# A new order of issue: measured lengths in the planner's list, and every stage's seeds searched anew

## The chip, the cores and the metric

The kernel runs on one core of a Trainium2 chip. Its engines are TensorE (PE, with PEld for its weight loads), VectorE (DVE), ScalarE (ACT), GpSimd (POOL) and SyncE (SP), which issues most of the DMAs. The metric is the device time of one execution, in microseconds (us).

## The reference

Two blocks in a row over 512 tokens of width 1024, in float32. Cut to what is computed:

```
hl = modulate(rms_norm(x), sh1, sc1)          # sh, sc, gt from silu(c) @ w_ada (24 MB)
q, k, v, f = split(hl @ w_in)                 # rope on q, k; 256 context rows join k, v
a = softmax(q1 k1) - lam * softmax(q2 k2)     # differential attention, 4 heads
mix = [rms_norm(a v), real(fft2(f)) @ w_fourier]   # 4 Fourier groups
x = x + gt1 * (mix @ w_out)
x = x + gt2 * hier_moe(modulate(rms_norm(x)))  # 32 experts, top 2 of 8 in one group, SwiGLU of 512
x = rms_norm(x, g_final)
# second block
p = rms_norm(x) @ w_in_2                      # 1024 -> 6152 columns
o_sb = stick_breaking_attention(...) * silu(gate)      # 8 heads of 64
o_g = gated_delta_rule(conv(...)) * silu(gate)         # 4 heads of 128, chunks of 64
y = (sig(m1) * (o_sb @ w_sb) + sig(m2) * (o_g @ w_gdn)) @ w_out_2
x = x + rms_norm(y)
```

## The kernel before

The whole work is one program in six stages, each recorded and then put in order by a planner. The stages, with the number of recorded operations, are the projections (1160: modulation from `w_ada`, norms, `w_in`, rope), the attention (901: Fourier mix, differential attention, the products with `w_out`, the router's weights), a short second stage (285: router and first gathers), the MoE (1661: 16 pairs of experts; every expert's weights are streamed, 64 x 3 DMAs of 1 MB), and two tail stages for the second block (2076 and 1867). All products are float32 kept by three fp32r products: a matrix is split into a high part (`wh`, `mh`, `w2h`, `bh`) and a rest (`wl`, `ml`, `w2l`, `bl`), and high x high, high x low and low x high are summed in PSUM. The high part is a cast, the rest a subtraction on DVE of some 128x512 or 128x1024 elements.

The order of issue is neither written by hand nor left to a compiler. A `Recorder` stands in the place of the engines (`s.nc.tensor`, `s.nc.vector` and so on); each call is kept with its operands. At the end of a stage `flush` gives each operation a priority (`rank`: the longest chain of costs behind it), changes the priorities by a list of random moves, one seed each, and runs `plan`, a list scheduler that plays the engines, buffers and DMAs by estimated costs (`cost_of`). The order that comes out is issued as it stands; each engine then runs its own operations strictly in that order and waits where an operand isn't there. Some operations may go to either of two engines (`alts`), and the planner chooses. All recorded instructions therefore carry one line, L1126, but for pairs of 64-column products (L852) and two scaling helpers (L794, L802).

The seeds stand in `ORDERS`, one row for each stage: (number of operations, share, keep, look, shy, seeds). The costs used to rank and to plan also decide what every old seed leads to: the first stage's outcome is carried into the next (`Recorder.before`).

Names used below: `ada` are blocks of `w_ada` (1 MB each), `kT` and `qT` rows of x (512 KB each) and later keys and queries, `pm` the modulation products in PSUM, `sc` silu(c); `sp` attention scores, `mx` their row maximum on DVE, `p` the weights, `pt` their transposes; `pf`, `pe`, `po` products of the Fourier transform with the tables `ab` and `dft`; `wout` blocks of `w_out` with rest `wl`; `py` an expert pair's output, `yt` and `yl` its weighted copy and rest, `x1` the residual; `w2`, `w2h`, `w2l` blocks of the second block's `w_in_2`. After the MoE stage a loop for overfull experts stands outside the recorder (0 rounds here): DVE copies `rk` just ahead of it, and all engines meet at it.

Of the kernel before, what the change touches and what calls it, by code (L numbers as in the profile page):

```python
# [537 lines left out]
def front(s, tc, ins, ctx, x1st, second, dump=None):  # L538
# [69 lines left out]
    if dump: dump("attn")  # L608
# [45 lines left out]
)  # L654


# [43 lines left out]
def _count(ap):  # L700
    n = 1
    for _, c in ap.ap[1:]:
        n *= c
    return n


class Recorder:
# [7 lines left out]
    before = ({}, {})  # L715
    turn = 0

    rate, switch = 360, 0

    LAT = {"tensor": {"tensor": 0, "vector": 196, "scalar": 197},  # L720
           "vector": {"tensor": 256, "vector": 127, "scalar": 160, "gpsimd": 200},
# [20 lines left out]

    def cost(self, eng, method, out, ins, kw):
        x = self.cost_of(eng, method, out, ins, kw)
        if self.switch and eng in ("vector", "scalar") and any(_count(a) > 64 and abs(a.ap[-1][0]) > 1 for a in (out, *ins)):

            x *= 1.75 if eng == "vector" else 2
        return x

    def cost_of(self, eng, method, out, ins, kw):  # L750
        n = _count(out)
        psum = any(str(a.space).endswith("PSUM") for a in ins + [out])
        if eng == "tensor":
            lhs = ins[0]
            if method == "transpose":
                return max(ins[0].ap[0][1] / 1.2, 50) + 3
            m = _count(lhs)
            if "32r" in str(lhs.dtype):
                return max(n, 256) / 2.4 + 2
            if m <= 32:  # L760
                return 19 + 0.43 * n
            if m <= 64:
                return 26 + 0.834 * n
            return max(4 * n, 512) / 2.4
        if eng == "scalar":
            return 0.833 * n + (60 if psum else 100) + (90 if kw.get("accum_out") is not None else 0) + \
                (84 if not isinstance(kw.get("scale", 1.0), float) else 0) + (90 if not isinstance(kw.get("bias", 0.0), float) else 0)
        if eng == "vector":
            n = max([n] + [_count(a) for a in ins])
            if method == "tensor_reduce":  # L770
                n = _count(ins[0])
            fast = method in ("tensor_copy", "tensor_scalar", "memset") and not psum
            return (0.52 if fast else 1.04) * n + 65 + 63 * sum(_count(a) == 1 for a in ins if n > 1)
        if eng == "gpsimd":
            if kw.get("op") is not None and "pow" in str(kw["op"]):
                return 300 + 165 * n
            if method == "scalar_tensor_tensor":
                return 100 + 1.4 * n
            return 200 + 2.1 * n if method == "tensor_tensor" else 150 + 0.9 * n
        return 60  # L780
# [136 lines left out]
    def plan(self, keep, look=0, shy=0):  # L917
# [9 lines left out]
        free = {e: self.before[0].get(e, 0.0) for e in self.ENGINES}  # L927
# [10 lines left out]
        dma, order, cols, sent = self.before[0].get("dma", 0.0), [], {}, []  # L938
        slots = {k: [(0.0, ())] * b for k, b in self.psum.items()}
        parked = {k: [] for k in slots}  # L940
        left, has, used, tiled = {}, set(), {}, False
        nexts = {k: 0 for k in slots}
        while len(order) < len(ops):
            best = None
# [13 lines left out]
            t, e = best  # L958
# [5 lines left out]
            op = heapq.heappop(now[e] if now[e] else later[e])[2]  # L964
# [49 lines left out]
            if e == "tensor":  # L1014


                x = 0
                for ph in (0.0, 0.5):
                    n = int(t / self.TICK + ph)
                    if n and cols.get((ph, n - 1), 0) < 3060:  # L1020
                        x = op.alts[e][1]
                small = "tile_position" in op.kw
                free[e] += x + (self.switch * (tiled != op.mode) if self.switch else 85 * (tiled and not small))
                tiled = op.mode if self.switch else small
                for ph in (0.0, 0.5):
                    n = int(free[e] / self.TICK + ph)
                    cols[ph, n] = cols.get((ph, n), 0) + op.cols
# [365 lines left out]
def phase_moe(s, last):  # L1393
    tc, nc, i = s.tc, s.nc, s.i
    right = "right"

    def load(e0):
        return s.pre.pop(e0) if e0 in s.pre else prefetch(s, e0, ahead=False)

    with ExitStack() as st:  # L1400
        s.ringD = st.enter_context(tc.tile_pool(name="ringD", bufs=RING - 17, reuse_waits="tile"))
        xp = st.enter_context(tc.tile_pool(name="xm", bufs=2, side=right, reuse_waits="tile"))
        ps = st.enter_context(tc.tile_pool(name="ps_m", bufs=8, space=PSUM, reuse_waits="tile"))
        s.nc = Recorder(nc, tc)
        s.nc.rate, s.nc.switch = 360, 95
        for x in s.ring:
            s.nc.tile(x)
        for e0 in range(0, 32, 2):
            got = s.got.pop(e0, None)
            if got is None:  # L1410
                got = gather(s, e0, s.rank, s.gx, ps, s.xs[e0 // 2 % 2])
            moe_pair(s, e0, got, xp, ps, load)
        last()
        s.nc.flush()
        s.nc = nc

    with ExitStack() as st:
        xp = st.enter_context(tc.tile_pool(name="xg", bufs=1, side=right, reuse_waits="tile"))
        ps = st.enter_context(tc.tile_pool(name="ps_g", bufs=8, space=PSUM, reuse_waits="tile"))
        wl = xp.tile([128, 512], F32, name="wl")  # L1420
        rk = xp.tile([128, 4, 32], F32, name="rk")
        nc.vector.tensor_copy(rk, s.rank)
        n = nc.values_load(s.nrounds[0:1, 0:1], min_val=0, max_val=512)
        with tc.For_i(0, n, 1):
            nc.vector.tensor_scalar(rk, rk, -float(s.cap), None, OP.add)
            for e0 in range(0, 32, 2):
                def load1(e0):
                    def ws(m, k, a):

                        nc.sync.dma_start(wl, expert_views(s, e0 + a)[m][:, k])  # L1430
                        return wl
                    return ws
                got = gather(s, e0, rk, xp, ps, s.xs[1], 1)
                moe_pair(s, e0, got, xp, ps, load1, paired=False)
    Recorder.before = ({}, {})
# [731 lines left out]
```

## Time and profile before

| | |
|---|---|
| three runs | 1327.03, 1330.16, 1330.43 us; median 1330.16 |
| the profiled execution | 1329.8 us, of which the span of the trace is 1328.1 us and 1.7 us lie around it |
| PE busy | 1233.0 us, 93% of the span, 7067 matmuls |
| DVE busy | 803.1 us, 60%, 1602 instructions |
| ACT, POOL busy | 529.3 us (40%), 109.7 us (8%) |
| granted TensorE clock, mean | 0.971 of full speed |
| moved by DMA | 297.5 MB, 224 GB/s over the span |

Times are microseconds from the start of the span. A row of the timeline gives the start, the time from the first start to the last end of the merged instructions, the engine, line and operation, output and inputs, the count, and in brackets how long the engine had been idle before and what released it. Matmuls are pipelined: the next may start while the last one is still shown, so that the distance of the starts, the pitch, is what a product costs. A row of the stretches gives the stretch, its length, busy time and count for each engine, the granted clock, the DMA share and GB/s.

### The profile page before, as it was taken

To read this page: it belongs to the slowest core of one execution; us is meant where nothing else is said; L and a number is where in the kernel's file an instruction comes from. 1 tells how busy PE (TensorE), PEld (TensorE's weight loads), DVE (VectorE), ACT (ScalarE), POOL (GpSimd) and SP (SyncE) were. 2 spreads that over 40 slices of the span, in tenths; PEclk is the share of its full clock that TensorE was granted. 3 is DMA by queue.
4 is the path that set the end of the run, shared out by engine and by line. 5 is a ranking of instruction groups with operands and counts; after the bars stand their busy time and mean duration, and the time that the engine had idled before them with its cause. 6 is when DMAs were issued, how large, how long until landed. Compare 5 with 4: busy or idle time off the path is not lost. (4 is left out here: it accounts for less than half of the span.)

```text
span 1328.1 us, 18293 instructions
## 1 busy us (share of the span) xinstructions
PE 1233.0 (93%) x7067; PEld 795.7 (60%) x7067; DVE 803.1 (60%) x1602; ACT 529.3 (40%) x1053; POOL 109.7 (8%) x115
## 2 busy tenths in 40 slices
PE   5999989899689999979998997899999999999997
PEld 3778667767333444424443332678777878888776
DVE  5788999867233443524434335769555676778674
ACT  4645367312112221311213212367554647458521
POOL 1213230021000000000000000102000100000010
PEclk9999999899689999989999999899999999999999
DMA  9976240118999999999999996222212221222421
GB/s 342 327 258 204 88 132 1 64 64 344 382 370 419 419 420 418 418 418 420 420 420 419 418 419 239 76 64 95 65 34 65 65 64 64 69 90 78 157 69 63
DMA packets 94228, 297.52 MB, mean 224 GB/s; under 512 B 10939, under 2 KB 44836, under 8 KB 69558
## 3 DMA queue, kind: packets, MB, share of 16 engines
q1 hardware_dynamic: 90166, 287.87, 56.3%
q0 software_dynamic: 3392, 6.31, 1.4%
q10 hardware_dynamic: 576, 2.10, 0.4%
q8 instruction: 57, 0.93, 0.3%
q14 instruction: 37, 0.30, 0.1%
HBM read 294.14 MB, written 6.31 MB: 226 GB/s over the span
## 5 line engine op out<-in xcount | busy, mean ns | idle before, releaser
L852 PE MATMUL pgu<-we,xT 128*64 128x512 f32 x1024 | 233.6, 604 | 7.7 <-DMA we<-in_w_gate_dram 7.7
L852 PEld LDWEIGHTS pgu<-we,xT 128*64 128x64 f32 x1024 | 73.2, 139 | 151.2 <-issue 146.1
L852 PE MATMUL py<-we,hT 128*64 128x512 f32 x512 | 121.6, 614 | 12.8 <-DMA we<-in_w_down_dram 9.5
L1126 PE MATMUL pgm<-bh,w2h 128*128 128x512 f32 x352 | 131.4, 407 | 0.0
L1126 PE MATMUL pgm<-bl,w2h 128*128 128x512 f32 x352 | 129.1, 402 | 0.0
L1126 PE MATMUL pgm<-bh,w2l 128*128 128x512 f32 x352 | 129.0, 402 | 0.0
L1126 DVE TENSOR_TENSOR x<-x,po 128x512 f32<-128x512 f32 x152 | 96.7, 683 | 36.1 <-PE po L1126 35.6
L1126 DVE SCALAR_TENSOR_TENSOR yt<-py,gs,gt 128x512 f32<-128x512 f32 x32 | 24.0, 751 | 115.9 <-PE py L852 110.4
L852 PEld LDWEIGHTS py<-we,hT 128*64 128x64 f32 x512 | 36.0, 141 | 83.3 <-issue 64.6
L1126 ACT CAST yh<-yt 128x512 fp32r<-128x512 f32 x32 | 19.8, 618 | 149.9 <-DVE yt L1126 149.7
L1126 PEld LDWEIGHTS pgm<-bl,w2h 128*128 128x128 f32 x352 | 66.1, 189 | 14.2 <-issue 0.2
L1126 PEld LDWEIGHTS pgm<-bh,w2h 128*128 128x128 f32 x352 | 66.0, 189 | 13.7 <-issue 0.3
L1126 PEld LDWEIGHTS pgm<-bh,w2l 128*128 128x128 f32 x352 | 65.6, 189 | 13.6 <-DVE w2l L1126 0.2
L1126 DVE TENSOR_TENSOR hs<-hs,pgu 128x512 f32<-128x512 f32 x16 | 11.0, 687 | 93.5 <-ACT hs L1126 93.5
L1126 ACT ACTIVATE xT<-px,mod 128x128 f32<-128x128 f32 x102 | 38.2, 462 | 66.4 <-PE px L1126 66.4
L1126 DVE TENSOR_TENSOR w2l<-w,w2h 128x2048 fp32r<-128x2048 f32 (+1 forms) x30 | 55.4, 1860 | 3.8 <-ACT w2h L1126 2.6
L1126 PE MATMUL po<-yh,PT 128*128 128x512 f32 x128 | 46.0, 437 | 10.9 <-ACT yh L1126 10.9
L1126 ACT ACTIVATE hs<-pgu 128x512 f32<-128x512 f32 x16 | 9.6, 598 | 103.4 <-PE pgu L852 102.5
L1126 POOL DMA_INDIRECT xs<-xnd,idx x16 | 17.0, 1065 | 390.2 <-DVE idx L1126 125.8
L1126 PE MATMUL po<-yl,PT 128*128 128x512 f32 x128 | 45.7, 428 | 2.3 <-DVE yl L1126 2.3
L1126 PEld LDWEIGHTS po<-yh,PT 128*128 128x128 f32 x128 | 24.9, 202 | 27.9 <-ACT yh L1126 15.6
L1126 ACT CAST w2h<-w 128x2048 fp32r<-128x2048 f32 (+1 forms) x20 | 32.8, 1650 | 20.7 <-PE pgm L1126 14.9
(562 smaller groups left out, 2584.3 us busy)
## 6 DMA issues: line engine op xcount, KB each, us to landing
we<-in_w_up_dram SPq DMA_DIRECT2D x64, 1024.0 KB
we<-in_w_down_dram SPq DMA_DIRECT2D x64, 1024.0 KB
we<-in_w_gate_dram SPq DMA_DIRECT2D x64, 1024.0 KB
ada<-in_w_ada_dram SPq DMA_DIRECT2D x24, 1024.0 KB
w<-in_w_in_dram SPq DMA_DIRECT2D x24, 1024.0 KB
win<-in_w_in_dram SPq DMA_DIRECT2D x8, 1024.0 KB
wout<-in_w_out_dram SPq DMA_DIRECT2D x4, 1024.0 KB
wo<-in_w_out_dram SPq DMA_DIRECT2D x4, 1024.0 KB
```

What stands on the lines that cost most here:

```text
L852: op.fn = lambda *a, **k: (real.matmul(*a, **k), real.matmul(*twin, **k))
L1126: x = op.alts[e][0](*op.args, **op.kw)
```

## The change

Nothing that is computed changes, and no instruction is added or taken away: 7067 matmuls before and after. What changes is the order of issue, and for 260 operations with a choice the engine. Three costs of the planner change: an fp32r product of 512 columns is priced at 230.6 instead of 215.3 ns; every change between tiling modes of TensorE (whole array, 64 columns, tiled) costs 95 ns in all stages, where before the MoE alone had that price and the others 85 ns on the way back to whole products; and strided operands of DVE and ACT are priced 1.75 and 2 times in all stages. Then new seeds are appended: 26 for the projections, 40 for the attention, 0, 3, 18 and 22 for the others.

```diff
@@ ORDERS (new numbers appended to five of six rows, two lines shown)
-        3928195128, 3886069083, 403543042)),
+        3928195128, 3886069083, 403543042, 1116446856, 3970406877, 624594825, 3832623241, 429937782,
...
@@ class Recorder
-    rate, switch = 360, 0
+    rate, switch = 360, 95
@@ cost
-        if self.switch and eng in ("vector", "scalar") and any(_count(a) > 64 and abs(a.ap[-1][0]) > 1 for a in (out, *ins)):
+        if eng in ("vector", "scalar") and any(_count(a) > 64 and abs(a.ap[-1][0]) > 1 for a in (out, *ins)):
@@ cost_of
             if "32r" in str(lhs.dtype):
-                return max(n, 256) / 2.4 + 2
+                return max(n, 256) / 2.22
@@ plan
-        left, has, used, tiled = {}, set(), {}, False
+        left, has, used, tiled = {}, set(), {}, 0
...
-                small = "tile_position" in op.kw
-                free[e] += x + (self.switch * (tiled != op.mode) if self.switch else 85 * (tiled and not small))
-                tiled = op.mode if self.switch else small
+                free[e] += x + self.switch * (tiled != op.mode)
+                tiled = op.mode
@@ the MoE stage
-        s.nc.rate, s.nc.switch = 360, 95
+        s.nc.rate = 360
```

In the order of issue, TensorE changes its tiling mode 36, 0, 16, 82, 110 and 8 times in the six stages before and 34, 0, 16, 94, 112 and 8 times after: 252 and 264.

The orders of issue below have one row for neighbours of one kind: line, operation, output and inputs, the output's shape, and the count. The recorder's line is L1126 before and L1138 after.

**The head of the projections.** SP's first DMA issues before (`ada_00` and `ada_01` are the first two blocks of `w_ada`):

```order
L1126 DMA ada_01_129<-in_w_ada_dram 128x8x256
L1126 DMA ada_00_128<-in_w_ada_dram 128x8x256
L1126 DMA kT<-in_x_dram 128x1024 x3
L1126 DMA cc<-in_c_dram 128x8
L1126 DMA cc<-in_c_ctx_dram 128x8
L1126 DMA qT<-in_x_dram 128x1024
```

and after:

```order
L1138 DMA rows<-in_b_ada_dram 16x128
L1138 DMA ada_00_128<-in_w_ada_dram 128x8x256
L1138 DMA kT<-in_x_dram 128x1024 x3
L1138 DMA cc<-in_c_dram 128x8
L1138 DMA cc<-in_c_ctx_dram 128x8
L1138 DMA ada_01_129<-in_w_ada_dram 128x8x256
```

One block of 1 MB has moved from ahead of the three `kT` to behind them; a small load stands first.

**The attention, around the rests of `w_out`.** DVE before, from `klz` to the second of two rests, `wl_1537` and `wl_1535` (`mx` is a row maximum, `f` and `p` work on attention weights):

```order
L1126 RECIPROCAL rc_1647<-sm_1667 128x2
L1126 TENSOR_TENSOR klz0_88<-kT_82,ks00_90 64x768
L1126 TENSOR_TENSOR wl_1537<-wout0_1_1533,wh_1536 128x1024
L1126 TENSOR_TENSOR ml1_1473<-fT_84,mh1_1472 128x4x128
L1126 SCALAR_TENSOR_TENSOR qs_1692<-qT_83,qs_1692 64x512
L1126 SCALAR_TENSOR_TENSOR f_1672<-rc_1647,nlam_69,sm_1667 128x1
L1126 TENSOR_REDUCE mx_1697<-sp_1696 128x1
L1126 SCALAR_TENSOR_TENSOR p_1666<-p_1666,f_1672 128x768
L1126 TENSOR_TENSOR wl_1535<-wout0_1_1533,wh_1534 128x1024
L1126 TENSOR_TENSOR klz1_89<-kT_82,ks01_91 64x768
```

and after:

```order
L1138 SCALAR_TENSOR_TENSOR p_1611<-p_1611,f_1617 128x768
L1138 TENSOR_REDUCE mx_1605<-sp_1604 128x1
L1138 TENSOR_TENSOR wl_1537<-wout0_1_1533,wh_1536 128x1024
L1138 TENSOR_REDUCE mx_1607<-sp_1606 128x1
L1138 TENSOR_TENSOR wl_1535<-wout0_1_1533,wh_1534 128x1024
L1138 TENSOR_REDUCE mx_1632<-sp_1631 128x1
```

Five instructions stood between the two rests, one stands there now. On TensorE the first transposes of attention weights (`pt`) came before right behind the scores:

```order
L1126 MATMUL sp<-ks_91,qs 128x256
L1126 MATMUL sp<-klz_89,qs 128x512
L1126 MATMUL sp<-klz_89,qs 128x256
L1126 MATMUL pt<-ident,p 128x128 x6
L1126 MATMUL pf<-ab,fT 128x256 x2
L1126 MATMUL pe<-dft,fh 128x258
```

and come after the change behind a run of Fourier products (`pe`, `po` from `dft`); the last rows of it are:

```order
L1138 MATMUL pe<-dft,fh 128x258 x2
L1138 MATMUL po<-dft,fl 128x258
L1138 MATMUL po<-dft,fh 128x258
L1138 MATMUL pe<-dft,fl 128x258
L1138 MATMUL po<-dft,fh 128x258
L1138 MATMUL po<-dft,fl 128x258
L1138 MATMUL po<-dft,fh 128x258 x2
L1138 MATMUL pe<-dft,fh 128x258 x2
L1138 MATMUL po<-dft,fl 128x258
L1138 MATMUL pt<-ident,p 128x128 x4
L1138 MATMUL pe<-dft,fl 128x258
L1138 MATMUL pt<-ident,p 128x128 x4
```

From the first to the last of that run, 29 such products have moved ahead of the first `pt`.

**The end of the MoE.** DVE before, from the blocks of the next stage's weights to the copy of `rk` ahead of the loop (`py_3745` and `py_3746` are the two halves of the last pair's output, `x_1468` the residual):

```order
L1126 CAST w2h<-w_2560_0_3757 128x512 x2
L1126 TENSOR_TENSOR w2l<-w_2560_0_3757,w2h 128x512 x4
L1126 CAST w2h<-w_2560_4_3760 128x512 x2
L1126 TENSOR_TENSOR w2l<-w_2560_4_3760,w2h 128x512 x2
L1126 SCALAR_TENSOR_TENSOR yt<-py_3745,gs,gt_1479 128x512
L1126 TENSOR_TENSOR w2l<-w_2560_4_3760,w2h 128x512 x2
L1126 TENSOR_TENSOR yl<-yt,yh 128x512
L1126 SCALAR_TENSOR_TENSOR yt<-py_3746,gs,gt_1479 128x512
L1126 TENSOR_TENSOR x_1468<-x_1468,po 128x512 x2
L1126 TENSOR_TENSOR yl<-yt,yh 128x512
L1126 TENSOR_TENSOR x_1468<-x_1468,po 128x512 x6
L1422 COPY rk<-rank 128x128
```

and after:

```order
L1138 TENSOR_TENSOR w2l<-w_2560_0_3757,w2h 128x512
L1138 SCALAR_TENSOR_TENSOR yt<-py_3745,gs,gt_1479 128x512
L1138 TENSOR_TENSOR w2l<-w_2560_0_3757,w2h 128x512 x2
L1138 TENSOR_TENSOR yl<-yt,yh 128x512
L1138 CAST w2h<-w_2560_4_3760 128x512
L1138 SCALAR_TENSOR_TENSOR yt<-py_3746,gs,gt_1479 128x512
L1138 TENSOR_TENSOR x_1468<-x_1468,po 128x512 x2
L1138 TENSOR_TENSOR yl<-yt,yh 128x512
L1138 TENSOR_TENSOR x_1468<-x_1468,po 128x512 x6
L1138 TENSOR_TENSOR w2l<-w_2560_0_3757,w2h 128x512
L1138 TENSOR_TENSOR w2l<-w_2560_4_3760,w2h 128x512 x4
L1434 COPY rk<-rank 128x128
```

The two weighted copies `yt` now stand ahead of most of the subtractions `w2l`; five of these stand behind the last addition to the residual and ahead of the copy of `rk`.

## Rows read from the trace of the kernel before

**Rows 1.** page, parts 1 and 2: busy times, granted clock, bandwidth by slice

```profile
PE 1233.0 (93%) x7067; PEld 795.7 (60%) x7067; DVE 803.1 (60%) x1602; ACT 529.3 (40%) x1053; POOL 109.7 (8%) x115
...
PEclk9999999899689999989999999899999999999999
...
GB/s 342 327 258 204 88 132 1 64 64 344 382 370 419 419 420 418 418 418 420 420 420 419 418 419 239 76 64 95 65 34 65 65 64 64 69 90 78 157 69 63
```

**Rows 2.** busy time of each engine by stage, TensorE clock, DMA share, GB/s

```profile
15.80:160.30 144.50, 143.89 (x755) 105.81 (x756) 116.47 (x250) 73.32 (x139) 34.57 (x30) 1.00 0.70 235
160.30:302.80 142.50, 127.71 (x639) 98.20 (x638) 120.74 (x206) 68.11 (x132) 25.27 (x23) 0.96 0.22 72
...
331.60:831.25 499.65, 451.73 (x2041) 188.24 (x2041) 197.79 (x371) 117.97 (x214) 14.87 (x14) 0.95 0.98 400
831.25:1052.30 221.05, 215.39 (x2202) 168.25 (x2202) 143.36 (x303) 120.54 (x276) 19.30 (x25) 0.98 0.22 70
1052.30:1320.80 268.50, 267.53 (x1254) 214.96 (x1253) 193.54 (x364) 136.80 (x268) 9.11 (x10) 1.00 0.23 78
```

**Rows 3.** timeline of SP, the first DMA issues

```profile
0.81 1.38 SPq L1126 DMA_DIRECT2D ada<-in_w_ada_dram  x2
2.23 3.06 SPq L1126 DMA_DIRECT2D kT<-in_x_dram  x3
```

**Rows 4.** timelines of ACT, then PE, at the start

```profile
12.57 1.06 ACT L1126 ACTIVATE hl<-kT 128x1024 fp32r<-128x1024 f32 x1 [10.48 <-DMA kT<-in_x_dram]
...
15.83 0.90 PE L1126 MATMUL ptr<-ident,kT 128*128 128x128 f32 x3 [15.83 <-DVE kT L794]
```

**Rows 5.** busy time by 20 us in the attention stage

```profile
160.00:180.00 20.00, 15.08 (x81) 11.33 (x80) 18.61 (x28) 14.41 (x27) 7.24 (x8) 1.00 0.98 299
...
220.00:240.00 20.00, 14.44 (x81) 12.00 (x80) 18.77 (x35) 10.37 (x22) 1.02 (x1) 0.85 0.14 49
...
260.00:280.00 20.00, 20.00 (x84) 12.74 (x83) 15.16 (x26) 6.92 (x14) 1.79 (x1) 1.00 0.26 90
```

**Rows 6.** timelines of PE, then DVE, around the longest PE wait of that stage

```profile
235.84 1.22 PE L1126 MATMUL po<-wl,mh 128*128 128x512 f32 x2 [4.53 <-DVE wl L1126]
236.86 0.63 PE L1126 MATMUL po<-wh,ml 128*128 128x512 f32 x1
237.29 0.63 PE L1126 MATMUL po<-wh,mh 128*128 128x512 f32 x1
...
230.09 1.21 DVE L1126 TENSOR_TENSOR wl<-wout,wh 128x1024 fp32r<-128x1024 f32 x1
...
234.57 1.22 DVE L1126 TENSOR_TENSOR wl<-wout,wh 128x1024 fp32r<-128x1024 f32 x1
```

**Rows 7.** busy time and clock behind that wait

```profile
235.80:240.80 5.00, 4.96 (x14) 3.91 (x15) 4.84 (x9) 1.61 (x3) 0.00 (x0) 0.51 0.60 211
```

**Rows 8.** chain of waits: TensorE products in one run of 72

```profile
1073.01 16.81 PE pgm L1126 x72
```

**Rows 9.** timeline of PE, a run of 32x32 products between 128x512 ones

```profile
1004.51 0.45 PE L1126 MATMUL pY<-inv,UL 32*32 32x32 f32 x32
1004.90 0.50 PE L1126 MATMUL pgm<-bh,w2l 128*128 128x512 f32 x1
1005.23 0.39 PE L1126 MATMUL pgm<-bh,w2h 128*128 128x512 f32 x1
```

**Rows 10.** timeline of DVE, then PE, at the end of the MoE stage

```profile
814.81 1.89 DVE L1126 TENSOR_TENSOR w2l<-w,w2h 128x512 fp32r<-128x512 f32 x3
...
821.07 0.75 DVE L1126 SCALAR_TENSOR_TENSOR yt<-py,gs,gt 128x512 f32<-128x512 f32 x1
...
824.97 3.08 DVE L1126 TENSOR_TENSOR x<-x,po 128x512 f32<-128x512 f32 x5 [0.57 <-PE po L1126]
...
809.67 7.09 PE L852 MATMUL py<-we,hT 128*64 128x512 f32 x32 [0.68 <-ACT hT L1126]
...
831.25 4.89 PE L1126 MATMUL pxt<-ident,x 128*128 128x128 f32 x28 [5.15 <-ACT qT L1126]
```

21 rows, old and new, of the table ORDERS are left out of this document.

## The prediction

> **What bounds the kernel now.** I read the page first. TensorE is busy for 1233.0 us of 1328.1, and its clock is granted in full in nearly all of the 40 slices [rows 1]. So the question of each stage is only what TensorE waits for there, and the table by stage answers it [rows 2]. In the projections it is busy for 143.89 of 144.5 us once it has begun at 15.8, in the last tail for 267.53 of 268.5. There no order of issue can give more than 0.6 and 1.0 us inside the stage. In the first tail 5.7 us are idle. In the MoE 48 us are idle, but the stage moves 400 GB/s with the DMA engines 98% busy; it is 200 MB of weights that set its length. The attention is left: TensorE is busy for 127.71 of 142.5 us, 14.8 us idle, with DVE busy for 120.74.
>
> The stretches of 20 us show where [rows 5]: from 160 to 180 DVE is busy for 18.61 and from 220 to 240 for 18.77, while TensorE has 15.08 and 14.44. By 260 to 280 TensorE is full and DVE is at 15.16. So the first 80 us of the stage run at DVE's pace and the rest at TensorE's. The longest single wait is 4.53 us, until 235.84, for `wl`, a rest of a block of `w_out` [rows 6]. DVE made the other rest at 230.09 and this one at 234.57; in between it did five other things, as the order shows. The granted clock then stands at 0.51, the 1.2 GHz level of TensorE's two, until 240.8 [rows 7].
>
> Ahead of all this lies a start of 15.83 us, with ACT waiting 10.48 us for the first `kT` [rows 4].
>
> **The change part by part.** *The new prices.* A product of 512 columns takes 16.81 / 72 = 233.5 ns [rows 8]; the list said 215.3 and now says 230.6. Around a run of 32x32 products the next 128x512 product takes 1005.23 - 1004.90 = 0.33 us instead of 0.2335 [rows 9]: 0.10 us for a change of tiling, for which the list now has 95 ns. Both prices come closer to the trace. They cost nothing by themselves; the order that follows is what is run.
>
> *Changes of tiling.* They go from 252 to 264. By the row these 12 are 1.2 us of TensorE. All 12 and more lie in the MoE (82 to 94), where 48 us of waiting for weights cover them: 0 there, +1.2 us if that cover were gone. The two more of the first tail are 0.2 us, the two fewer of the projections the same: 0 together. The Trainium skill, TensorEngine Tiling (Array Packing), Key Properties, says that a change of mode, not of tile, drains TensorE. The 0.10 us above agrees with it, and by this rule alone a list with 12 more changes would be the worse one, by 1.2 us in place of 0.
>
> *The head of the projections.* The 2 MB of `ada` are issued from 0.81 and the three `kT` behind them from 2.23 [rows 3]. In the change one block stands behind the `kT`. At the first slice's 342 GB/s [rows 1] the 1.05 MB are 3.1 us; the small load now at the head costs an issue of about 0.7 us, as each of the first two `ada` takes, though one `ada` less is ahead. I take -2.5. TensorE is full behind its first product, so what it gains at its start stays to the end of the stage. The bounds: -4 (all of 3.1 and one of the waits for scale vectors), and +1, if the second block, now late, is what TensorE waits for.
>
> *The attention.* No change of tiling happens here. The two rests now stand one `mx` apart on DVE, and TensorE's first product with the late one comes behind scores of other heads. That frees the 4.53 us, and what came of it: the 14 matmuls of the 5 us behind it at half the clock [rows 7] ran at a pitch of 237.29 - 236.86 = 0.43 us [rows 6], against 0.2335, so some 12 x 0.2 = 2.4 us. Together 6.9. What is late next: DVE is at 18.77 of 20 there, and the wait of TensorE is in the end for DVE's sum. I leave 1.9 us of it standing (a subtraction of 1.2 us and its read) and take -5. The bounds are the whole idle time of TensorE, -14.8 [rows 2], and +5.5 (the first rival). The Trainium skill, TensorE: Matmul & The Clock Gate, part 1, states that the gate sets the clock by how busy the array has just been. The 0.51 behind the wait agrees; a sum that left the clock out would have -2.6 here in place of -5.
>
> *The end of the MoE.* The stream of weights begins when the attention has freed its buffers and has the same length, so the stage moves as a whole with what comes ahead of it. Its last output is there at 809.67 + 7.09 = 816.76 [rows 10]. Before, DVE takes the second `yt` at 821.07, since eight subtractions stand ahead. After, one `yt` (0.75), two subtractions (1.26), a rest and a cast (about 1.2) stand behind 816.76, so the second `yt` begins near 819.9, and the additions end 1.2 us earlier than 824.97 + 3.08. But five subtractions of 1.89 / 3 = 0.63 us follow, 3.15 us, and only then the copy at which DVE comes to the loop where all engines meet. That is +1.9 us on TensorE's restart at 831.25. Bounds: -1 (the subtractions fit between the additions' waits; 0.57 us idle is there now), and +3.2.
>
> *The tails.* The second stage keeps its order. The first tail begins with the same chain of norms behind the loop, and behind it TensorE is full; the last tail ends with the same products. Both could lose, as there is little to gain: 0, bounds -2 and +4.5, a wait as long as the attention's longest [rows 6].
>
> The sum is -2.5 - 5 + 1.9 = -5.6 us, from the profiled execution's 1329.8 to 1324.2 us; that execution is 0.4 us below the median of 1330.16. A change under 0.3%, 4 us, is hardly to be told from none here.
>
> **The rivals.**
>
> *DVE starves behind filler (slower).* After the change 29 Fourier products of TensorE stand ahead of the first `pt`, where none stood before. At the pitch of their like, some 0.12 us, half of a product of 512 columns [rows 8], that is 3.5 us, and two more groups of scores are ahead too, 8 products or 2 us: `pt` may come 5.5 us later. If ACT and DVE have nothing else, DVE loses these 5.5 us in a stretch in which it is the bound. It decides if DVE's idle time in the stage grows above today's 142.5 - 120.74 = 21.8 us. For it: 18.61 busy of 20 in just that stretch [rows 5]. Against it: several row maxima are in reach there. Time: 1329.8 - 2.5 + 5.5 + 1.9 = 1334.7.
>
> *The wait moves.* DVE's sum stays 120.7 and TensorE waits elsewhere as long: 0 in the attention. For it: 14.8 us of idle time lie in many small waits beside the long one. Time: 1329.2.
>
> *The attention fills up.* The Fourier work covers the first 80 us and neither engine idles: not all of the 14.8 us can go, since DVE's 120.74 begins behind the first scores and ends ahead of the last products; I put 11, three quarters, as an estimate. Time: 1329.8 - 2.5 - 11 + 1.9 = 1318.2.
>
> *The prices don't reach the time.* The list is truer, but seeds chosen against it give only another order of the same waits; the head gains nothing, as TensorE needs silu(c), which stands behind `kT` in both, and the late second block. Time: 1329.8 + 1.9 = 1331.7, no change.
>
> **How the numbers follow.** The forecast has 0.50, the filling up 0.14, the wait that moves 0.16, the prices without effect 0.08, the starved DVE 0.12. The forecast's own range is -11 to -2, 1319 to 1328, so that about 0.05 of its 0.50 falls within 4 us of the median. Faster by over 0.3%: 0.45 + 0.14 = 0.59, and 0.01 of the third: 0.60. Within: 0.05 + 0.15 + 0.06 = 0.26. Slower: 0.12 + 0.02 = 0.14. The range takes in both ends: 1329.8 - 2.5 - 14.8 = 1312.5 at the low one, with nothing lost at the loop, and 1334.7 with another 1.3 (the bound of the loop's meeting) at the high one: 1312 to 1336. What lies outside is mostly the low end of a full attention with a gain at the head, and losses of the tails beside a starved DVE.
>
> **What would show it.** The head: the first `hl` of ACT near 10 instead of 12.57, and TensorE's first product near 13.3. The attention: no wait of 4.5 us for `wl`, no stretch at half the clock behind it, idle time of TensorE near 10 instead of 14.8, the stage 137 us long. The MoE: length unchanged within 2 us. Its end: 3 us of `w2l` behind the last `x` and a restart of TensorE 16.4 instead of 14.5 us behind the last `py`. The tails: 489 us as before. I am wrong if the attention is longer than 142 us, or if waits of over 2 us appear in the tails.

## The result, and the profile after

The changed kernel took 1339.48 us (median of 4, 1336.01 to 1341.25) where the kernel before took 1330.01 (median of 4): the ratio is 1.0082, with a 95% interval from 1.0056 to 1.0107. It is slower; 1324.2 had been forecast, and the range ended at 1336. A second set of runs, `after2` below, gave 1.0069 [1.0052, 1.0085].

The profiled execution took 1336.01 us, its span is 1334.0. The page, TensorE's busy time and the granted clock, against [rows 1]:

```profile
PE 1237.3 (93%) x7067; PEld 790.0 (59%) x7067; DVE 805.6 (60%) x1604; ACT 527.6 (40%) x1053; POOL 110.7 (8%) x113
...
PEclk9999999999799999999999998899999999999999
```

Both are almost as they were, so that the page alone tells nothing. The table by stage does (the columns of [rows 2]):

```profile
14.79:165.51 150.72, 145.51 (x756) 106.01 (x757) 118.46 (x254) 73.30 (x137) 38.19 (x26) 1.00 0.69 231
165.51:302.50 136.99, 126.48 (x639) 95.81 (x638) 122.10 (x206) 67.31 (x130) 25.88 (x24) 0.99 0.23 74
...
331.25:831.99 500.74, 450.57 (x2041) 184.37 (x2041) 196.60 (x371) 115.87 (x211) 14.11 (x14) 0.96 0.97 397
831.99:1058.75 226.76, 219.85 (x2202) 169.51 (x2202) 143.02 (x301) 122.19 (x280) 20.13 (x26) 0.97 0.22 71
1058.75:1326.71 267.96, 267.88 (x1254) 214.34 (x1253) 194.71 (x360) 136.37 (x272) 5.89 (x9) 1.00 0.24 79
```

The projections begin 1.0 us earlier and end 5.2 us later: TensorE, which had 0.6 us idle in that stage, has 5.2. The attention is 5.5 us shorter. The first tail is 5.8 us longer.

What TensorE waits for in the projections, from its waits there (what released it, us in all, times, longest); before there was one of 0.6 us after the start:

```profile
PE pq L1138 <- POOL hl L1138: 1.6, 1, 1.6
PE pm L1138 <- DMA ada<-in_w_ada_dram: 1.1, 1, 1.1
PE pq L1138 <- ACT hh L1138: 0.8, 1, 0.8
PE pk L1138 <- DVE cs L1138: 0.8, 1, 0.8
PE pq L1138 <- DVE mods L1138: 0.4, 1, 0.4
PE pv L1138 <- DVE tmp L815: 0.4, 1, 0.4
```

Six waits, for three engines and a DMA: no one thing is late. The start itself, ACT and PE against [rows 4]:

```profile
11.59 1.06 ACT L1138 ACTIVATE hl<-kT 128x1024 fp32r<-128x1024 f32 x1 [9.50 <-DMA kT<-in_x_dram]
...
14.79 1.07 PE L1138 MATMUL pm<-ada,sc 128*32 128x256 f32 x6 [14.79 <-DVE sc L1138]
```

The first `kT` comes 1.0 us earlier, not 2 to 3. And the end of the MoE, timelines of SP, DVE, ACT and PE, against [rows 10]:

```profile
824.49 0.40 SPq L1138 DMA_DIRECT2D w<-in_w_in_dram  x1
...
823.74 3.09 DVE L1138 TENSOR_TENSOR w2l<-w,w2h 128x512 fp32r<-128x512 f32 x5
826.75 0.22 DVE L1434 COPY rk<-rank 128x128 f32<-128x128 f32 x1
...
831.57 1.06 ACT L1138 ACTIVATE qT<-x 128x1024 f32<-128x1024 f32 x1 [12.48 <-SPq L1436]
...
831.99 5.57 PE L1138 MATMUL pxt<-ident,x 128*128 128x128 f32 x28 [10.47 <-SPq L1436]
```

VectorE's five late subtractions are there, but `rk` is done at 826.97 and ScalarE restarts 4.6 us later, released by SP. Seven us before that restart SP had issued a block of 1 MB.

The table holds the lengths of the stages in all profiles that follow, each from its first product on TensorE to that of the next stage. The kernels are told below.

| kernel | start | proj. | attention | second | MoE | tail 1 | tail 2 |
|---|---|---|---|---|---|---|---|
| before | 15.8 | 144.5 | 142.5 | 28.8 | 499.6 | 221.0 | 268.5 |
| after | 14.8 | 150.7 | 137.0 | 28.7 | 500.7 | 226.8 | 268.0 |
| after2 | 14.4 | 151.3 | 137.2 | 28.8 | 499.1 | 225.6 | 268.0 |
| p_only | 14.0 | 151.3 | 142.8 | 28.8 | 498.5 | 221.7 | 268.5 |
| a_only | 16.2 | 143.2 | 139.5 | 28.8 | 500.6 | 220.8 | 268.5 |
| m_only | 16.1 | 143.6 | 143.6 | 28.8 | 502.8 | 222.1 | 268.5 |
| t_only | 16.1 | 143.2 | 142.4 | 28.8 | 498.1 | 225.9 | 268.5 |
| m_mid | 16.0 | 143.4 | 142.7 | 28.8 | 499.3 | 220.9 | 268.5 |
| wl_early | 16.0 | 144.1 | 142.9 | 28.8 | 498.9 | 220.8 | 268.5 |
| head | 14.5 | 147.4 | 142.3 | 28.8 | 495.0 | 220.9 | 268.5 |
| p_eng | 14.5 | 150.6 | 142.8 | 28.8 | 499.7 | 220.8 | 268.5 |
| t_eng | 16.5 | 144.0 | 142.6 | 28.8 | 498.9 | 235.6 | 268.3 |
| a_eng | 15.7 | 143.2 | 145.8 | 28.8 | 498.3 | 220.9 | 268.5 |
| t_fill | 16.2 | 143.7 | 141.2 | 28.8 | 499.7 | 232.3 | 268.0 |
| t_w2l | 16.2 | 143.1 | 143.7 | 28.8 | 499.8 | 228.5 | 268.6 |
| best | 15.7 | 143.3 | 140.4 | 28.8 | 500.3 | 221.0 | 267.9 |
| prices | 16.1 | 167.5 | 183.4 | 28.7 | 505.4 | 231.5 | 278.4 |
| seeds | 14.2 | 160.6 | 148.2 | 28.8 | 502.1 | 233.2 | 270.8 |

With the same order of the stage, the projections repeat within 1.4 us, the attention within 2.5, the first tail within 1.3, the last within 0.6, and the MoE, where the weights stream, only within 6 (495.0 to 500.6 with the order of before). The start is 15.7 to 16.5 with the old head and 14.0 to 14.8 with the new one. A difference of a whole run under 3 us is therefore read here by the stage. The profile of before has longer projections (144.5) than its copies (143.1 to 144.1), so that the loss against a usual run of before is a little larger than the two profiles show.

### The profile page after: what moved, and what is told of

Same layout as the page of the kernel before. It is cut to its first block, busy times and chain, and to the rows that moved or that the text cites. A ratio compares the mean times of both kernels' runs of the same rounds, so it can differ in the third digit from the quotient of the medians.

```text
span 1334.0 us, 18314 instructions
## 1 busy us (share of the span) xinstructions
PE 1237.3 (93%) x7067; PEld 790.0 (59%) x7067; DVE 805.6 (60%) x1604; ACT 527.6 (40%) x1053; POOL 110.7 (8%) x113
## 5 line engine op out<-in xcount | busy, mean ns | idle before, releaser
L865 PEld LDWEIGHTS pgu<-we,xT 128*64 128x64 f32 x1024 | 72.7, 140 | 148.2 <-issue 142.4
L1138 PE MATMUL pgm<-bh,w2l 128*128 128x512 f32 x352 | 135.7, 405 | 0.0
L1138 PE MATMUL pgm<-bh,w2h 128*128 128x512 f32 x352 | 135.2, 405 | 0.0
L1138 PE MATMUL pgm<-bl,w2h 128*128 128x512 f32 x352 | 134.3, 403 | 0.0
L1138 DVE TENSOR_TENSOR x<-x,po 128x512 f32<-128x512 f32 x152 | 97.2, 682 | 48.3 <-PE po L1138 48.1
L865 PE MATMUL py<-we,hT 128*64 128x512 f32 x512 | 116.6, 596 | 6.4 <-ACT hT L1138 4.2
L1138 DVE SCALAR_TENSOR_TENSOR yt<-py,gs,gt 128x512 f32<-128x512 f32 x32 | 24.0, 751 | 115.2 <-PE py L865 114.7
L1138 ACT CAST yh<-yt 128x512 fp32r<-128x512 f32 x32 | 19.8, 618 | 159.2 <-DVE yt L1138 159.1
L1138 PEld LDWEIGHTS pgm<-bh,w2l 128*128 128x128 f32 x352 | 66.3, 189 | 14.8 <-DVE w2l L1138 1.0
L1138 PEld LDWEIGHTS pgm<-bl,w2h 128*128 128x128 f32 x352 | 66.1, 189 | 13.9
L1138 PEld LDWEIGHTS pgm<-bh,w2h 128*128 128x128 f32 x352 | 66.1, 189 | 13.8 <-issue 0.6
L1138 DVE TENSOR_TENSOR w2l<-w,w2h 128x2048 fp32r<-128x2048 f32 (+1 forms) x30 | 55.4, 1859 | 7.3 <-ACT w2h L1138 4.1
L1138 ACT ACTIVATE xT<-px,mod 128x128 f32<-128x128 f32 x101 | 38.0, 460 | 54.3 <-PE px L1138 52.0
L1138 PE MATMUL po<-yh,PT 128*128 128x512 f32 x128 | 45.2, 429 | 12.6 <-ACT yh L1138 12.6
L1138 DVE TENSOR_TENSOR hs<-hs,pgu 128x512 f32<-128x512 f32 x16 | 11.0, 685 | 69.6 <-ACT hs L1138 69.6
L1138 ACT ACTIVATE hs<-pgu 128x512 f32<-128x512 f32 x16 | 9.6, 597 | 103.0 <-PE pgu L865 98.9
L1138 POOL DMA_INDIRECT xs<-xnd,idx x16 | 16.3, 1018 | 373.1 <-DVE idx L1138 145.6
L1138 PE MATMUL po<-yl,PT 128*128 128x512 f32 x128 | 44.7, 423 | 2.0 <-DVE yl L1138 2.0
L1138 PEld LDWEIGHTS po<-yh,PT 128*128 128x128 f32 x128 | 23.7, 193 | 33.6 <-ACT yh L1138 20.2
L1138 DVE TENSOR_TENSOR hp<-hs,pgu 128x512 f32<-128x512 f32 x16 | 16.9, 1056 | 35.1 <-PE pgu L865 35.0
```

The lines of the kernel that those rows point to most:

```text
L865: op.fn = lambda *a, **k: (real.matmul(*a, **k), real.matmul(*twin, **k))
L1138: x = op.alts[e][0](*op.args, **op.kw)
```

## The experiments

**One stage at a time.** The recorded operations are planned twice, with the list and seeds of before and with those of the change, each with what its own last stage left over. Each stage's order is then taken from one or the other; the numbers name the six stages.

```diff
+MIX = (1, 0, 0, 0, 0, 0)
...
+        order = got[1 - MIX[where]][0]
```

`p_only` is (1, 0, 0, 0, 0, 0), `a_only` (0, 1, 0, 0, 0, 0), `m_only` (0, 0, 0, 1, 0, 0), `t_only` (0, 0, 0, 0, 1, 0). The four ran together; before had 1327.92 us there.

p_only: 

> Every stage is planned twice, by the list and seeds of before and by those of the change, and each stage's order of issue is taken from one or the other; here the projections alone have the order of the change. Theory S (each stage's loss stands by itself): TensorE's waits in the projections come along, so that this stage ends some 4.8 us later (165.1 against 160.3) and nothing behind it changes: 1330 + 4.8 = 1335. Theory C (work was only carried over the border): the projections' loss is what the attention gains, since what the one leaves unfinished on VectorE the other had to do; then with the attention's old order the end of the attention lies within 1.5 us of before: 1330 to 1331.5.

a_only: 

> The attention alone has the order of the change. Theory S: the stage is 137 instead of 142.5 us, no wait of 4.5 us for wl and no half clock behind it: 1330 - 5.5 = 1324.5. Theory C: the attention's gain was the projections' late end, and the stage keeps 141 us or more: 1328.5 to 1330.

m_only: 

> The MoE alone has the order of the change. Theory S: from the last py to TensorE's restart 17 instead of 14.5 us; the weight stream itself ended 1.2 us earlier in relation to the stage's begin, so +1.1 in all: 1331. Theory C: MoE unchanged once the stages ahead are as before: 1330.

t_only: 

> The first tail alone has the order of the change. Theory S: the 4 us of small waits between 970 and 1058 are the order's own and stay: +4 to +5.8: 1334 to 1336. Theory C: they came from weights that were loaded late because the MoE's end issued one block late; with the MoE as before the stage is as before: 1330 to 1331.

Measured: `p_only` 1331.57 us (1.0040 [1.0018, 1.0062]), `a_only` 1325.34 (0.9970 [0.9952, 0.9988]), `m_only` 1334.94 (1.0050 [1.0023, 1.0078]), `t_only` 1332.38 (1.0039 [1.0020, 1.0058]). Three lose alone, one wins alone: theory S in the main. The four differences make +3.7 - 2.6 + 7.0 + 4.5 = +12.6 us, near the 9.5 of the change. Projections and first tail bring their loss along (151.3 and 225.9 us). `m_only` loses more than theory S had for it; its MoE is 502.8 us long where the same order takes 500.7 and 499.1 in the two profiles of the change, so how much of the 7.0 us is the order's own is not shown. And one thing is carried over after all: the attention's new order takes 139.5 to 140.4 us behind the old projections (theory S had 137, theory C 141 or more) and 137.0 to 137.2 behind the new ones. Of the gain of 5.5 us, 2.1 to 3.0 are its own order's.

**The end of the MoE.** `m_mid` is `m_only` with the five subtractions moved on VectorE:

```diff
+            late = [order[at[i]] for i in (1651, 1654, 1656, 1658, 1660)]
+            order = [x for x in order if x not in late]
+            n = [op.idx for op, e in order].index(1616) + 1
+            order[n:n] = late
```

> As m_only (the MoE alone in the order of the change), but the five subtractions w2l that stood behind the last additions to the residual stand right behind the second yt. VectorE has the same work ahead of its copy of rk. Theory D (the forecast's: VectorE's backlog is what all engines wait for at the loop): rk ends as late as in m_only behind the last py (11.9 us) and the restart stays 16.5 us behind the last py: 0 against m_only. Theory B (the loop's branch on SP waits for all DMAs that were issued, and the last 1 MB block for the next stage was issued late, since it waits for the buffer that the late subtraction reads): SP issues that block some 5 us earlier, and ScalarE restarts within 1.6 us of rk instead of 4.6: 2.5 to 3.5 us less than m_only.

Measured: 1330.41 us beside 1328.75 of before (1.0031 [1.0004, 1.0057]). First SP, DVE, ACT and PE of `m_only`, then the same of `m_mid`:

```profile
827.82 0.39 SPq L1177 DMA_DIRECT2D w<-in_w_in_dram  x1
...
830.08 0.22 DVE L1469 COPY rk<-rank 128x128 f32<-128x128 f32 x1
...
834.72 1.06 ACT L1177 ACTIVATE qT<-x 128x1024 f32<-128x1024 f32 x1 [12.29 <-SPq L1471]
...
834.94 5.67 PE L1177 MATMUL pxt<-ident,x 128*128 128x128 f32 x28 [10.11 <-SPq L1471]
```

```profile
820.65 0.39 SPq L1183 DMA_DIRECT2D w<-in_w_in_dram  x1
...
825.88 0.23 DVE L1475 COPY rk<-rank 128x128 f32<-128x128 f32 x1
...
828.21 1.06 ACT L1183 ACTIVATE qT<-x 128x1024 f32<-128x1024 f32 x1 [9.98 <-SPq L1477]
...
830.25 5.95 PE L1183 MATMUL pxt<-ident,x 128*128 128x128 f32 x28 [5.74 <-ACT qT L1183]
```

The last `py` ended at 818.18 and 813.98. So `rk` began 11.9 us behind it in both, as theory D would have it all that counts; ScalarE's restart went from 16.5 to 14.2 us behind it. It follows the last 1 MB block: 6.9 and 7.6 us after its issue (7.1 and 6.1 in `after` and `after2`). SP's own waits from 800 to 836 us, first before, then two of `m_only`, then `m_mid`:

```profile
SPq L1424 <- SPq L1424: 3.4, 4, 2.9
...
SPq L1177 <- DVE w2l L1177: 11.4, 1, 11.4
SPq L1471 <- SPq L1471: 5.5, 1, 5.5
...
SPq L1477 <- SPq L1477: 3.7, 4, 3.0
```

In `m_only` SP waits 11.4 us, before it can issue the block, for a subtraction that had been put off: the block's buffer is free when that one has read the old content. Then it stands 5.5 us at the loop, where it waits for the semaphores of its DMA queues one after another; the one it stands at is the one that this block signals. For ScalarE theory B holds, at 2.3 us where 2.5 to 3.5 was expected. For TensorE it does not: its first product behind the loop comes 16.8 and 16.3 us behind the last `py`, 14.5 before. The move gave it back 0.5 of 2.3 us, and what holds it for the rest is open. `rk`, 0.7 us later than before (11.9 and 11.2 us), may have a part in it.

**The wait for `wl` alone.**

```diff
+            x = order.pop(at[169])
+            order.insert(at[171], x)
```

> The kernel before, with one instruction moved: VectorE makes the rest wl_1535 right ahead of wl_1537 instead of five instructions behind it. Theory W (the forecast's term): TensorE's wait of 4.53 us shrinks below 1 us and the 5 us at half the clock behind it go: the attention is 136 to 138 us long, 1330 - 5 = 1325. Theory T (VectorE is the bound of that stretch, so the wait only moves): the attention keeps 141 us or more, within 1.5 us of before.

Measured: 1331.23 us beside 1328.75 (1.0015 [0.9992, 1.0038]); the attention takes 142.9 us. From TensorE's waits in it:

```profile
PE pt L1181 <- DVE oT L1181: 4.5, 1, 4.5
```

The 4.53 us of [rows 6] are there to the tenth, at another product, behind another instruction of VectorE. Theory T.

**The head alone.** SP's first eleven loads in the order of the change, all else as before:

```diff
...
+            for n, i in zip(at, (3, 42, 6, 4, 5, 0, 1, 43, 7, 92, 2)):
+                order[n] = ops_[i]
```

> The kernel before, with SP's first loads alone in the order of the change (the second block of w_ada behind kT, the small load first). Theory H (the forecast's term): ScalarE's first hl is 2 to 3 us earlier than 12.57 and the projections end 2.5 us earlier: 1327.5. Theory L (a load behind a block of 1 MB shares the queues with it and gains little): the first hl is 1 us earlier, as in the change, TensorE's first product some 1 us earlier, and the stage ends within 1.5 us of before, or later if the second block is now missed.

Measured: 1330.41 us beside 1328.75 (1.0017 [0.9995, 1.0039]). The first `hl` is at 11.20, the first product at 14.46 instead of 15.83. Then TensorE's timeline:

```profile
21.80 0.33 PE L1182 MATMUL ptr<-ident,qT 128*128 128x128 f32 x1 [1.75 <-ACT qT L1182]
22.68 1.07 PE L1182 MATMUL pm<-ada,sc 128*32 128x256 f32 x4 [0.55 <-DMA ada<-in_w_ada_dram]
```

The load of `qT` now stands behind the block that was moved, and TensorE waits for it. The stage ends at 14.46 + 147.40 = 161.86, 1.5 us later than in the profile of before and 1.4 to 2.9 later than in all the profiles with that order. Theory L, at its worse end. The head alone makes the projections 147.4 us long, about half of the way to the 150.6 to 151.3 of the whole new order.

**Order and engines.** `p_eng`, `t_eng` and `a_eng` take one stage's new order, but leave each operation on its old engine:

```diff
+            was = {op.idx: e for op, e in got[1][0]}
+            order = [(op, was[op.idx]) for op, e in order]
```

p_eng: 

> The projections in the order of the change, but each operation on the engine on which it was before (91 had changed). Theory E (the engines cost the time, above all a subtraction hl that went to GpSimd): most of the 5 us are gone, the stage ends within 1.5 us of 160.3: 1330 to 1331. Theory O (the order itself makes TensorE wait in a stage in which it was full): the stage still ends 3 us or more later: 1333 or more.

t_eng: 

> The first tail in the order of the change, but each operation on the engine on which it was before (53 had changed). Theory O (the order: TensorE comes to the chunked delta rule's products with no filler between): the stage stays 4 us or more above the 221 us of before, with waits of 0.3 to 0.6 us at the same places. Theory E (the engines): within 1.5 us of 221.

a_eng: 

> The attention in the order of the change, but each operation on the engine on which it was before (41 had changed). Theory O (the order of TensorE, with the Fourier products as filler ahead of the first pt, gives the gain): the stage stays 2 us or more below the 142.5 us of before. Theory E (order and engines are one solution, and either without the other is worse, as in the first tail): the stage is 143 us or longer.

Measured: `p_eng` 1333.18 us beside 1328.75 (1.0031 [1.0011, 1.0051]), its projections 150.6 us: the engines were not the loss. `t_eng` 1342.78 beside 1329.28 (1.0102 [1.0066, 1.0138]), the first tail 235.6 us, ten longer than with the engines that belong to the order. `a_eng` 1330.08 beside 1329.6 (1.0002 [0.9983, 1.0021]), the attention 145.8: with the old engines the order that won is 3.3 us worse than that of before. In these two stages order and engines are one solution.

**Prices and seeds apart.** `prices` is the changed kernel with the seeds of before, `seeds` the kernel before with the seeds of the change. The cut shows `prices` against the changed kernel.

```diff
-        3928195128, 3886069083, 403543042, 1116446856, 3970406877, 624594825, 3832623241, 429937782,
...
+        3928195128, 3886069083, 403543042)),
```

prices: 

> The new prices with the seeds of before in all six stages. Read by stage. Theory P (the truer prices make the better order): no stage is longer than before by over 1.5 us, and the attention is 139 us or less. Theory F (an order is only as good as the seeds searched for its prices): old seeds under new prices are as good as no search, and the full stages (projections, tails) are 3 us or more longer each: 1340 or more.

seeds: 

> The old prices with the new seeds in all six stages. Theory P: the prices were what mattered, the attention stays at 142 us. Theory F: the appended seeds, searched under other prices, do nothing reliable here; the full stages are 3 us or more longer each: 1340 or more.

Measured: `prices` 1417.98 us (1.0656 [1.0623, 1.0689]), `seeds` 1367.32 (1.0297 [1.0266, 1.0328]), before 1329.28. By the stages in `prices`, projections and attention:

```profile
15.80:183.30 167.50, 150.05 (x755) 107.41 (x755) 113.09 (x249) 73.96 (x139) 28.48 (x26) 0.96 0.67 222
183.30:366.60 183.30, 146.15 (x637) 105.69 (x637) 133.76 (x229) 65.56 (x124) 10.61 (x12) 0.89 0.12 39
```

TensorE is idle for 17 us of the one and 37 of the other. Theory F, and far beyond its 10 us: with the seeds of before, the truer list gives an order that is 89 us longer. The appended seeds won back all but 9.5 of it under the new list, and under the old one lost 38. No run has either list without any seeds, so what of the 89 us is lost search and what the list itself would cost is not shown.

**The first tail's waits.** In `t_only`, `after` and `after2`, twelve products of TensorE start 0.14 to 0.63 us later than the usual pitch of their shapes, in all about 4 us, at the same twelve places and each time within 0.04 us; before there are two or three, under 1 us. `t_fill` and `t_w2l` change two of these places.

```diff
+            for at, n in ((899, 3),):
+                p = pe.index(at)
+                some = [i for i in pe[p:] if fill(i)][:n]
...
+            p = pe.index(1730)
+            some = [i for i in pe[:p] if fill(i)][-3:]
```

t_fill: 

> The first tail in the order of the change, as t_only, with six of TensorE's own 128x512 products moved: three stand ahead of the transpose poT that waited 0.62 us more than its pitch, and three, issued before, are held back to stand ahead of the product pvn that waited as long. No work is added. Theory G (gaps of filler: the small chained products stand next to each other and TensorE waits for ScalarE and VectorE between them): both places lose their wait, so 1.0 to 1.3 us of the stage's loss go, and the other ten gaps stay as they are to 0.1 us. Rival: the operands are late for another reason and come later with the products, so that the gaps stay or move.

Measured: 1339.92 us beside 1329.6 (1.0075 [1.0050, 1.0101]), the stage 232.3 us, 6.4 longer than `t_only`. At the first place the 0.62 us went, and 0.44 came up behind it. At the second, DVE and PE:

```profile
1052.70 0.69 DVE L824 TENSOR_SCALAR sq<-pgm 128x512 f32<-128x512 f32 x1 [3.94 <-PE pgm L1217]
1053.31 2.28 DVE L1217 TENSOR_TENSOR w2l<-w,w2h 128x2048 fp32r<-128x2048 f32 x1
1055.51 0.34 DVE L1217 SCALAR_TENSOR_TENSOR r<-pst,neG,nat 128x128 f32<-128x128 f32 x1
...
1055.91 0.58 PE L1217 MATMUL pvn<-r,X 128*128 128x128 f32 x1 [3.24 <-DVE r L1217]
```

The product held back is read by VectorE (`sq`), which waits for it, and in its queue stand the long subtraction `w2l` and the `r` that TensorE needs. Theory G fails: the filler made the wait 3.2 us. This also showed what stands ahead of `r`, and so the next run moved `w2l`:

```diff
+            x = order[at[2075]]
+            order.insert(at[1491] + 1, x)
+            order.pop(at[2075])
```

t_w2l: 

> The first tail in the order of the change, as t_only, with one instruction of VectorE moved: the last rest w2l of 128x2048 (2.28 us), which stands right ahead of the residual r that TensorE's product pvn waits for, stands behind it and the four updates that follow. Theory Q (the waits come from long preparations that stand in the queue of VectorE ahead of the chain): the waits of 0.62 and 0.38 us at pvn and pst go, so 0.8 to 1.0 us of the stage's loss, and the other ten gaps stay. Rival: the wait only moves to the next link, as with the filler, and the stage is as long as in t_only.

Measured: 1337.2 us beside 1329.0 (1.0056 [1.0036, 1.0076]), the stage 228.5 us, 2.6 longer than `t_only`. The wait at `pvn` shrank from 0.62 to 0.19 us, about half of what theory Q had in all; that at `pst` stayed as it was. And from TensorE's waits:

```profile
PE po L1182 <- DVE ss L1182: 2.2, 1, 2.2
```

The next link of the chain now stands behind the 2.28 us. The rival holds for the time. Where the twelve waits could be had back is left open; at two places it wasn't by one move.

**The change again.**

> The changed kernel once more, for a second profile of it: the one shown is the fastest of its four runs. Stages whose loss is the order's own (projections, first tail, attention) come back to within 1 us; what differs between the two profiles then lies in the MoE, where the weights stream.

Measured: 1337.32 us beside 1329.0, ratio as above. Projections, attention and first tail come back within 0.6, 0.2 and 1.2 us; the MoE differs by 1.6. Its profiled run took 1333.51 us, the other three 1337 to 1338; where these 4 us lie no profile shows.

**What the runs point to.** `best` takes the attention and the last tail from the change and the other stages from before (MIX = (0, 1, 0, 0, 0, 1)).

> The attention and the last tail in the order of the change, the other four stages in that of before. Theory S (the stages' gains stand by themselves): attention 3 to 5.5 us shorter, last tail 0.5 us shorter: 1324 to 1326.5 where before has 1329 (ratio 0.996 to 0.998). Rival: the attention's gain was chance of one set of runs, and nothing is left beyond 1 us.

Measured: 1324.39 us (median of 12) beside 1329.28 (17): 0.9963 [0.9946, 0.9981]. It beats both kernels. The last tail is 267.9 us, as in the change; but the old order took 268.0 there in `t_fill`, and `a_only` alone had 0.9970, so what the last tail adds isn't shown. The attention's gain is 2.1 us in this profile.

## Why the prediction was wrong

**The step that failed** is the price of what has no price: "TensorE is full behind its first product, so what it gains at its start stays to the end of the stage", with a bound of +1, and the first tail at 0. I read from [rows 2] that a full stage could give nothing, and took the new order to differ little from the old one there. A full stage has little to win and much to lose. The projections lost 6.2 to 6.8 us inside and ended 5.0 to 5.4 later, counted with their earlier start; the first tail lost 4.6 to 5.8. By stage the profile of the change makes -1.0 + 6.2 - 5.5 + 1.1 + 5.8 - 0.5 = +6.1 us where -5.6 was forecast: head and projections came to +5.2 instead of -2.5, the tails to +5.3 instead of 0, and these two are more than the whole miss. The rest of the 9.5 us lies in executions that have no profile. My bound of +4.5 for the tails was the right size for one of two stages and carried a chance of next to nothing in the range. `prices` shows what was behind it: the old order came from its seeds and its prices together, and with new prices the same seeds lead elsewhere. The order after is not the old one improved, but another search's result.

*The new prices* come closer to the trace, as said; that "the order that follows is what is run" was right, and I priced only the pieces of it that I had followed in the rows.

*The head* was forecast at -2.5. It made the start 1.0 and 1.4 us earlier in the two profiles of the change, and alone it costs 1.5 us by the end of the stage: with 1.05 MB less ahead of the first `kT`, ScalarE's first `hl` began 1.0 to 1.4 us earlier where the 342 GB/s of [rows 1] made it 3.1, and `qT` came late. I had counted what the moved block stood in front of, and not what it now stands in front of.

*The attention* was forecast at -5 and gave -5.5 and -5.3: the right size for the wrong reason, and by luck, since its own order gives 2.1 to 3.0 of it and the rest came only behind the new projections. The wait for `wl` was only where VectorE's lateness came to light: in `wl_early` it moved, and the clock stood at 0.50 behind it there too (238 to 243 us). The stage gained as a whole: TensorE's idle time went from 14.8 to 10.5 us and the clock from 0.96 to 0.99, as the sum of many waits, and only together with its engines (`a_eng`). Which part of the order does it is open. The rival of a VectorE starved behind filler did not come: its idle time fell from 21.8 to 136.99 - 122.10 = 14.9 us.

*The end of the MoE* was forecast at +1.9 behind the last `py`; TensorE's restart came 831.99 - 814.84 = 17.2 us behind it, where it was 14.5, so +2.7 (+1.6 in `after2`). The size was near, the mechanism only in part: ScalarE waited not for VectorE's backlog but for a load which VectorE set free late, at a loop that waits for all loads; with the load moved ahead again, TensorE still lost 1.8 of 2.3 us.

*Changes of tiling*, 12 more, lie in the MoE, which in the two profiles of the change is no longer than its own spread (499.1 and 500.7); its weights' cover holds as far as that can tell. *The last tail*, full as well, kept its length, -0.5.

## What to carry to other kernels

An order of issue found by a search belongs to the costs under which it was found: here a truer cost list with the old seeds was 89 us longer. Take the outcome of a new search stage by stage, and keep a stage's order only if it is shorter. In a stage where the bounding engine is full, count a new order as a loss until its waits are read. And a wait that is the longest of its stretch is not its cause: take it away alone before its length is counted as a gain.

## What was not expected of the hardware

The first loads did not come by bytes ahead of them: with 1.05 MB less ahead of the first `kT`, ScalarE's first `hl` began at 10.83 to 11.59 us in six profiles, and at 12.41 to 13.22 in the twelve with the old head. That is 1.6 us in the mean, where the rate of the first slice would have given 3.1; why, no run shows. And a block of 1 MB that SP issued last or nearly last ahead of the loop held SP there: in the four profiles with the MoE's new order ScalarE restarted 6.1 to 7.6 us after its issue.
